# State space branch with features on partitions and its norm applied later; first weights in contiguous blocks; key rotation issued between the halves of the query latent

## The chip, the cores and the metric

The kernel runs on one core of a Trainium2 chip. A core has five engines that work side by side and meet through semaphores: TensorE (PE, matrix products; its weight loads are shown apart as PEld), VectorE (DVE), ScalarE (ACT), GpSimd (POOL) and SyncE (SP, which here only issues DMAs). Data lies in SBUF, a memory of 128 partitions; products land in PSUM, in banks of 128 partitions by 512 floats. Each engine works through its own list of instructions in order.

The metric is the device time of one execution, in microseconds (us). Times are medians of several runs; a profile is one further execution.

## The reference: what is computed

Two layers of a decoder trunk on 512 tokens of width 1024, in float32. In each layer a normed input goes through one wide projection, whose columns feed three branches: a state space scan (Mamba-2 SSD), latent attention (MLA) and a gated delta rule (GDN). Each branch is projected to the model's width and weighted by a sigmoid gate; their sum goes through an output projection and a feed-forward part. The branch that the change is about, cut to what matters:

```python
def ssd_mixer(z, xbc, dt_raw, conv_w, conv_b, dt_bias, a_log, d_skip, norm_g):
    xbc = silu(causal_dwconv(xbc, conv_w) + conv_b)
    xs, bm, cm = split(xbc)                       # 16 heads of 64; 2 groups of 8 heads; state 128
    dt = softplus(dt_raw + dt_bias)
    a = -exp(a_log)
    y = ssd_chunked(xs * dt[..., None], dt * a, bm, cm)
    y = y + d_skip[:, :, None] * xs
    y = y * silu(z)
    return rmsnorm(y, norm_g)                     # over the 512 features of each group

def ssd_chunked(X, dA, Bm, Cm):                   # chunks of 128 tokens
    A_cum = cumsum(dA)
    L = exp(where(tril, A_cum[l] - A_cum[s], -inf))
    CB = einsum('ln,sn->ls', Cc, Bc)
    y_diag = einsum('ls,ls,sp->lp', CB, L, X)
    states = einsum('ln,l,lp->pn', Bc, exp(A_cum[-1] - A_cum), X)
    # scan over the chunks: h = h * exp(A_cum[-1]) + states
    y_off = einsum('ln,pn,l->lp', Cc, h_prev, exp(A_cum))
    return y_diag + y_off
```

## The kernel before

**Number formats.** The large (dense) products are three products each (`mm3`, L182 to L184) of operands split in a high and a low part of type fp32r. A weight tile comes from DRAM by a DMA on SP's queue (`weights_raw`, L161, two buffers `wraw`), ACT casts the high part (`split_half`, L154), DVE subtracts it for the low part (L155). The small products of the scans are plain fp32. `dense_F` makes a product with features on the output's partitions (weights held in the array, 512 tokens streaming), `silu_T`'s product has tokens on the partitions (token blocks held, 512 weight columns streaming).

**Buffers.** PSUM has four banks `acc` for dense products, three banks `sm` for small ones and one, `yt`. SBUF tiles come from pools with a fixed number of buffers by name: `tok` (four of 128x2048), `eE` (four), `wk0` to `wk3` (one each), `ft4` (two), `st` (two). A tile that takes a buffer over waits until its last reader is done.

**Order.** The program is written stage by stage, and a scheduler reorders each engine's list by priority and by readiness; weights' casts are marked as high priority. So the list of PE holds dense products of the next stage between the small products of a scan. Around the SSD branch the program has, in each layer: `ssd_group(0)`, the decays of the delta rule (`gdn_decays`, which uses `seg_exp` and the `eE` buffers too, and writes `d_e`), half of the attention's output projection, `ssd_group(1)`, the other half, `gdn_matrix` for two halves of the heads, `gdn_blocks` (inverses of 32x32 blocks on DVE, by way of DRAM: `d_n`, then `d_x`, which PE waits for at L891), the SSD branch's output projection with steps of the inverse (L891 to L929) between its rows, then the rest of the delta rule.

**The SSD branch.** `step_sizes` makes the cumulative sums `cum`, stores them as rows in DRAM (`d_c`), and exponentials of them (`dec`), the step `dtq` and the skip factor `dsk`. One call of `ssd_group(g)` does 8 heads:

- Projections of B, C (features on partitions), and of x in two 256-wide pieces (features on partitions), convolved (`conv`), then transposed by PE (L720) and copied by ACT (L721) so that `xs` has tokens on partitions; z by `silu_T` with tokens on partitions.
- For each of the four chunks t: `seg_exp` loads the chunk's cumulative sums of four heads into an `eE` buffer, broadcast to all partitions (L448, 256 KB), and ACT takes the exponentials (L450, L451); twice for 8 heads. PE makes C·B (L733), DVE masks it (L735) and multiplies it into both `eE` (L737). `xd` is x times the step (L739). Eight products `py` (L742) hold a head's 128x128 decay matrix in the array and stream its 64 columns of `xd`. `y` is the skip term (L744) plus `py` (L745). For t > 0 the state's share `po` (L748, the C block held, the state's 512 columns streaming) is scaled by `dec` (L750) and added (L751). For t < 3 the state is brought forward (L754, L756, L759 to L762). y is multiplied into `z` (L764), and ACT squares it and sums along the row (L766).
- At the end POOL takes the root (`rsq`, L258 and L259), DVE scales the four rows of z (L770), PE transposes all of it (L775) and `split_gain` (ACT L254, DVE L255) applies the gain and makes the high and low parts `yh`, `yl` for the output projection.

**The attention's start.** `query_latent(0)` and `(1)` project the query's latent in two halves, and sums of its squares come from PE (L513). `rope` rotates the key: four DMAs on ACT's queue copy it with halves swapped (L519 to L521), DVE multiplies by cosine and sine. The queries' own rotations come later and end in `qps` (L591), which the scores (L625) read.

**Loads at the start of a layer.** `front_raw` (L306 to L310) loads the weights of the first small projections, four pieces of 128 x 704, each row a piece of a longer row in DRAM.

Of the kernel before, what the change touches and what calls it, by code (L numbers as in the profile page):

```python
# [10 lines left out]
F32 = mybir.dt.float32  # L11
# [9 lines left out]
P = 128  # L21
# [13 lines left out]
ROWS = ('ssd_dt_bias', 'gdn_dt_bias', 'ssd_a_log', 'gdn_a_log', 'ssd_d')  # L35
# [20 lines left out]
def hybrid_kernel(ctx, tc, a, out, depth=2, taps=None):  # L56
# [4 lines left out]
    def mk(pl, shape, dt, tag, bufs=None):  # L61
        return pl.tile(shape, dt, tag=tag, name=f"{tag}_{next(uid)}", bufs=bufs)
# [30 lines left out]
    def sm_bank():  # L93
        return mk(ps_sm, [P, 512], F32, "sm")
# [4 lines left out]
    ct = mk(cst, [P, NBLK * P + 104], F32, "ct")  # L99
# [195 lines left out]
    def load_params(ly, rows=True):  # L295
        pc = mk(sp, [P, 155], F32, "pc", 2)
        sync.dma_start(pc, a["pcols"][ly])
        prow = mk(sp, [P, 64], F32, "prow", 2)
        if rows:
            load_rows(prow, ly)  # L300
        return pc, prow
# [49 lines left out]
    for ly in range(depth):  # L351
# [5 lines left out]
        sconv_b, g_n1, g_ssd, g_q, g_kv, g_gdn, g_n2 = 0, 12, 20, 28, 32, 34, 35  # L357
# [32 lines left out]
        d_c = mk(dr, [T, 24 * P], F32, "d_c", 2)  # L390

        def step_sizes():
# [35 lines left out]
            sync.dma_start(d_c.rearrange("t (n l) -> (t n) l", l=P), rows)  # L428
            dec = mk(sp, [P, 3, T, 24], F32, "dec")
# [8 lines left out]
            dsk = mk(sp, [P, 16], F32, "dsk")  # L438
            dve.tensor_scalar(dsk, prow[:, 48:64], 0.25, None, ALU.mult)
# [63 lines left out]
        query_latent(0)  # L503
        ckh, ckl = latent(lp, ck_tok, 256, g_kv, "ck")
        ps = sm_bank()
        for t in range(T):
            pe.transpose(ps[:, t * P : (t + 1) * P], kr_tok[:, t], ident)
        kd = mk(lp, [P, S], F32, "mix", 8)
        act.copy(kd, ps)
        query_latent(1)  # L510
        ps = sm_bank()
        for t in range(T):
            pe.matmul(ps[:, t : t + 1], cq_sq[0][:, t * P : (t + 1) * P], ones[:, 0:1], start=True, stop=True)  # L513
        q_rs = mk(sp, [P, T], F32, "qrs")
        rsq(q_rs, ps[:, :T], 1.0 / 512, EPS)

# [10 lines left out]

        kpe = rope(kd)
# [4 lines left out]
        dve.tensor_tensor(kps[64:], kpe[64:], f32(kph[64:]), ALU.subtract)  # L533

# [162 lines left out]
        def ssd_group(g, yh, yl):  # L697
            h0 = 8 * g
            xs = mk(br, [P, T, 512], F32, "tok", 4)
            z = mk(br, [P, T, 512], F32, "tok", 4)  # L700
# [13 lines left out]
            for cp in range(2):  # L714
                for j, pj in enumerate(dense_F(weights(w_in, O_XBC + 512 * g + 256 * cp, 256, D), tiles(256), D, xh, xl)):
                    xf = mk(br, [P, S], F32, "ft4", 2)
                    conv(pj, 4 * g + 2 * cp + j, xf)
                    ps = sm_bank()
                    for t in range(T):
                        pe.transpose(ps[:, t * P : (t + 1) * P], xf[:, t * P : (t + 1) * P], ident)  # L720
# [4 lines left out]
            ss = mk(sp, [P, T], F32, "sss")  # L725
            st = None
            for t in range(T):
# [10 lines left out]
                xd = mk(br, [P, 512], F32, "wk0")  # L738
                dve.tensor_tensor(hv8(xd), hv8(xs[:, t, :]), bc_last(dtq[:, t, h0 : h0 + 8], 64), ALU.mult)  # L739
                py = sm_bank()  # L740
                for h in range(8):
                    pe.matmul(py[:, h * 64 : (h + 1) * 64], e2[h // 4][:, h % 4, :], xd[:, h * 64 : (h + 1) * 64], start=True, stop=True)  # L742
                y = mk(br, [P, 512], F32, "wk1")
                dve.tensor_tensor(hv8(y), hv8(xs[:, t, :]), bc_last(dsk[:, h0 : h0 + 8], 64), ALU.mult)  # L744
                dve.tensor_tensor(y, y, py, ALU.add)  # L745
                if t > 0:
                    po = sm_bank()
                    pe.matmul(po, ctl[:, tok], st, start=True, stop=True)  # L748
                    y2 = mk(br, [P, 512], F32, "wk2")
                    dve.tensor_tensor(hv8(y2), hv8(po), bc_last(dec[:, 0, t, h0 : h0 + 8], 64), ALU.mult)  # L750
                    dve.tensor_tensor(y, y, y2, ALU.add)  # L751
                if t < T - 1:
                    xe = mk(br, [P, 512], F32, "wk3")
                    dve.tensor_tensor(hv8(xe), hv8(xd), bc_last(dec[:, 1, t, h0 : h0 + 8], 64), ALU.mult)  # L754
                    pst = sm_bank()
                    pe.matmul(pst, btok[:, t, :], xe, start=True, stop=True)  # L756
# [7 lines left out]
                dve.tensor_tensor(z[:, t, :], z[:, t, :], y, ALU.mult)  # L764
                jk = mk(br, [P, 512], F32, "wk2")
                act.activation(jk, z[:, t, :], AF.Square, accum_out=ss[:, t : t + 1])  # L766
            rs = mk(sp, [P, T], F32, "srs")
            rsq(rs, ss, 1.0 / 512, EPS)
            for t in range(T):
                dve.tensor_scalar(z[:, t, :], z[:, t, :], rs[:, t : t + 1], None, ALU.mult)  # L770
            for c in range(4):
                k = 4 * g + c
                ps = y_bank()
                for t in range(T):
                    pe.transpose(ps[:, t * P : (t + 1) * P], z[:, t, c * P : (c + 1) * P], ident)  # L775
                split_gain(yh[k], yl[k], ps, col(g_ssd + k))
                tap(f"yssd{k}", f32(yh[k]))
# [24 lines left out]
        def gdn_matrix(u):  # L802
# [26 lines left out]
            nt = mk(br, [P, T, 4, P], F32, "tok", 4)  # L829
# [14 lines left out]
        def gdn_blocks():  # L844
# [4 lines left out]
            wk = mk(br, [P, 2, 32, 32], F32, "tok", 4)  # L849
# [20 lines left out]
        def gdn_inverse(ms, blocks):  # L870
# [4 lines left out]
            X = mk(br, [P, 2, 4 * T, 64], F32, "tok", 4)  # L875
# [63 lines left out]
        def gdn_unit(u, kT, ork, cc, cd, Yt, yh, yl):  # L939
# [18 lines left out]
            v = mk(br, [P, T, 512], F32, "tok", 4)  # L958
            gz = mk(br, [P, T, 512], F32, "tok", 4)
# [314 lines left out]
def lay_out(inputs):  # L1274
# [4 lines left out]
    cols = np.concatenate([v[n].reshape(depth, -1, P) for n in PARAMS], axis=1)  # L1279
# [4 lines left out]
    res["w_front"] = np.ascontiguousarray(w.reshape(depth, KD, P, NF).transpose(0, 2, 1, 3)).reshape(depth, P, KD * NF)  # L1284
# [18 lines left out]
```

## Time and profile before

| | |
|---|---|
| median of 3 runs | 2335.56 us (2330.37 to 2335.94) |
| the profiled execution | 2337.45 us |
| its span, first to last instruction | 2335.7 us |
| mean granted TensorE clock | 0.994 of full speed |
| mean share of the DMA engines' time on q1 (the loads) | 33.0% |

The page divides the span in 40 slices. Each digit below is the busy share of one slice in tenths.

```profile
PE   8999999999999999999999999999999999999998
DVE  7776657765675458767767765667756645677668
ACT  5666744333443345545656667443334434545545
PEclk9999999989999999999999999999999999999999
DMA  4223533442322443233132235334423224333231
```

A busy PE is not PE at its peak: matmuls overlap and their ends are modelled, so the durations in the groups add up to more than the time they take. Where a time per matmul is needed, the distance from one start to the next is the better number. The page counts an fp32 product as two records.

### The profile page before, as it was taken

How to read it: one execution, taken by the hardware profiler on the slowest of the kernel's cores; microseconds unless marked ns; L12 is line 12 of the kernel's file. 1: busy time of each engine (PE TensorE's matmuls, PEld its weight loads, DVE VectorE, ACT ScalarE, POOL GpSimd, SP SyncE). 2: the span in 40 equal slices, each digit the busy share in tenths (PEclk: the TensorE clock that was granted, in tenths of full speed). 3: DMA queues.
4: the chain of work that ended last, by engine and by line, in shares of the span. 5: the costliest groups of instructions: out<-in, count | busy, mean ns of one | idle time of the engine just before them, and what ended most of it. 6: DMA issues, size and time to landing. Idle time of an engine off the chain costs nothing.

```text
span 2335.7 us, 32023 instructions
## 1 busy us (share of the span) xinstructions
PE 2294.3 (98%) x11814; PEld 1889.9 (81%) x11814; DVE 1586.4 (68%) x3116; ACT 1177.1 (50%) x2455; POOL 59.5 (3%) x74
## 2 busy tenths in 40 slices
PE   8999999999999999999999999999999999999998
PEld 7878788878887888888888787888788878888886
DVE  7776657765675458767767765667756645677668
ACT  5666744333443345545656667443334434545545
POOL 0000000000000000000010000000000000000000
PEclk9999999989999999999999999999999999999999
DMA  4223533442322443233132235334423224333231
GB/s 136 83 69 91 171 100 111 117 136 73 86 75 66 146 152 101 72 126 115 41 106 68 82 92 170 100 106 138 118 82 86 68 78 157 127 117 100 90 109 46
DMA packets 208703, 239.85 MB, mean 103 GB/s; under 512 B 33889, under 2 KB 157473, under 8 KB 208545
## 3 DMA queue, kind: packets, MB, share of 16 engines
q1 hardware_dynamic: 205344, 233.07, 33.0%
q10 hardware_dynamic: 3200, 4.72, 0.8%
q8 instruction: 93, 1.52, 0.3%
q14 instruction: 66, 0.53, 0.1%
HBM read 221.41 MB, written 11.63 MB: 100 GB/s over the span
## 4 chain that ended last, share of the span: by engine, by line
PE 88%; DVE 6%; DMA 2%; ACT 2%; POOL 1%; issue 1%; ACTq 0%; SPq 0%; DVEq 0%; POOLq 0%
PE acc L182 23%; PE acc L184 22%; PE acc L183 22%; PE sm L184 2%; PE sm L182 2%; PE sm L183 2%; DVE wlo L155 1%; PE sm L742 1%; DMA eE<-d_c 1%; PE sm L645 1%; DVE tok L858 1%; DVE gQ L857 1%; PE sm L1015 1%; POOL gms L259 1%; PE yt L661 1%
## 5 line engine op out<-in xcount | busy, mean ns | idle before, releaser
L155 DVE TENSOR_TENSOR wlo<-wraw,whi 128x512 fp32r<-128x512 f32 (+1 forms) x552 | 376.6, 686 | 420.8 <-ACT whi L154 401.5
L154 ACT CAST whi<-wraw 128x512 fp32r<-128x512 f32 (+1 forms) x552 | 339.9, 618 | 593.1 <-PE acc L183 383.6
L184 PE MATMUL acc<-xh,wlo 128*128 128x512 f32 (+1 forms) x1248 | 486.8, 390 | 0.0
L182 PE MATMUL acc<-xh,whi 128*128 128x512 f32 (+1 forms) x1248 | 486.1, 390 | 0.0
L183 PE MATMUL acc<-xl,whi 128*128 128x512 f32 (+1 forms) x1248 | 485.1, 389 | 0.0
L184 PEld LDWEIGHTS acc<-xh,wlo 128*128 128x128 f32 x1248 | 235.8, 189 | 44.9 <-issue 0.3
L183 PEld LDWEIGHTS acc<-xl,whi 128*128 128x128 f32 x1248 | 235.8, 189 | 44.4 <-DVE xl L255 0.4
L182 PEld LDWEIGHTS acc<-xh,whi 128*128 128x128 f32 x1248 | 235.3, 189 | 43.7 <-ACT xh L254 0.4
L182 PE MATMUL acc<-yh,whi 128*128 128x512 f32 x384 | 151.9, 399 | 0.0
L183 PE MATMUL acc<-yl,whi 128*128 128x512 f32 x384 | 151.4, 394 | 0.0
L184 PE MATMUL acc<-yh,wlo 128*128 128x512 f32 x384 | 151.2, 394 | 0.0
L686 DVE SCALAR_TENSOR_TENSOR ckl<-acc,pc,ckl 128x511 f32<-128x511 f32 (+2 forms) x168 | 120.2, 743 | 15.5 <-ACT ckl L682 8.2
L154 ACT CAST whi<-wr 128x512 fp32r<-128x512 f32 x128 | 79.5, 621 | 66.7 <-PE acc L184 31.1
L184 PE MATMUL acc<-whi,xl 128*128 128x512 f32 (+1 forms) x288 | 111.2, 386 | 0.0
L183 PE MATMUL acc<-wlo,xh 128*128 128x512 f32 (+1 forms) x288 | 111.1, 386 | 0.0
L182 PE MATMUL acc<-whi,xh 128*128 128x512 f32 (+1 forms) x288 | 110.3, 385 | 0.0
L182 PE MATMUL acc<-whi,yh 128*128 128x512 f32 x256 | 99.7, 389 | 0.0
L184 PE MATMUL acc<-whi,yl 128*128 128x512 f32 x256 | 99.7, 389 | 0.0
L183 PE MATMUL acc<-wlo,yh 128*128 128x512 f32 x256 | 99.6, 389 | 0.0
L155 DVE TENSOR_TENSOR wlo<-wr,whi 128x512 fp32r<-128x512 f32 x128 | 86.0, 686 | 12.2 <-ACT whi L154 11.4
L182 PEld LDWEIGHTS acc<-yh,whi 128*128 128x128 f32 x384 | 71.7, 188 | 16.7 <-ACT yh L254 1.7
L183 PEld LDWEIGHTS acc<-yl,whi 128*128 128x128 f32 x384 | 72.2, 188 | 15.2 <-issue 1.0
(418 smaller groups left out, 4531.0 us busy)
## 6 DMA issues: line engine op xcount, KB each, us to landing
wraw<-in_w_in_dram SPq DMA_DIRECT2D x144, 512.0 KB, 3.6
wraw<-in_w_up_dram SPq DMA_DIRECT2D x64, 512.0 KB, 3.6
wr<-in_w_down_dram SPq DMA_DIRECT2D x32, 1024.0 KB, 5.0
eE<-d_c SPq DMA_DIRECT2D x48, 256.0 KB, 3.9
wraw<-in_w_mla_out_dram SPq DMA_DIRECT2D x16, 512.0 KB, 3.4
eE<-d_e SPq DMA_DIRECT2D x32, 256.0 KB, 3.2
wraw<-in_w_ssd_out_dram SPq DMA_DIRECT2D x16, 512.0 KB, 3.4
wraw<-in_w_gdn_out_dram SPq DMA_DIRECT2D x16, 512.0 KB, 3.3
```

Of the source, the lines that this page charges most:

```text
L154: act.copy(hi, raw)
L155: dve.tensor_tensor(lo, raw, f32(hi), ALU.subtract)
L182: pe.matmul(o, ah, bh, start=start, stop=False, skip_group_check=more)
L183: pe.matmul(o, ah, bl, start=False, stop=False, skip_group_check=more)
L184: pe.matmul(o, al, bh, start=False, stop=stop, skip_group_check=more)
L259: pool.tensor_tensor(o, o, (exp if exp is not None else nhalf)[:, : o.shape[1]], ALU.pow)
L645: pe.transpose(ps[:, n : n + P], pn[t][:, kb * P : (kb + 1) * P], ident)
L661: pe.matmul(o, v_h, th[:, c : c + w], start=kb == 0, stop=False)
L686: dve.scalar_tensor_tensor(acc[:, d:], ps[:, : S - d], taps_[3 - d], acc[:, d:], ALU.mult, ALU.add)
L742: pe.matmul(py[:, h * 64 : (h + 1) * 64], e2[h // 4][:, h % 4, :], xd[:, h * 64 : (h + 1) * 64], start=True, stop=True)
L857: dve.tensor_tensor(pd, bc_last(nb[:, m, m + 1 :], m + 1), bc_mid(xb[:, m, : m + 1], 31 - m), ALU.mult)
L858: dve.tensor_tensor(xb[:, m + 1 :, : m + 1], xb[:, m + 1 :, : m + 1], pd, ALU.add)
```

## The change

Three things change. The sums and products that make up the output stay the same, in another layout.

1. *The SSD branch keeps features on partitions.* The convolved x stays as it is (`xf`), is scaled by the skip factor in place (a column per feature now, read from the parameters), and its transpose goes from PSUM straight into `xd`, multiplied by the step. z is projected by `dense_F`. The products `py` hold a head's 128x64 piece of `xd` and stream the decay matrix; odd heads write PSUM partitions 64 to 127. `po` is four products. The factor exp(cum), which was a scalar per partition, now varies along the row, and is loaded from a new DRAM tile `d_p` into the buffers `wk0` and `wk1`. The sum of squares over features is now a sum over partitions, made by two adds on DVE and a product with ones into the bank `yt`. The root goes to DRAM (`d_r`) and comes back broadcast in the function `normed`, which multiplies z by gain and root and splits it. `normed` is called after the attention's output projection for the first group, and between the two calls of `gdn_matrix` for the second. `tok` gets a fifth buffer.
2. *The first weights* lie in DRAM as four contiguous blocks per layer.
3. *The key's rotation* is issued before `query_latent(1)`, not after it.

```diff
-        sync.dma_start(raw, a["w_front"][ly][:, 2 * q * NF : 2 * (q + 1) * NF])
+        sync.dma_start(raw, a["w_front"][ly, q])
...
+            prows = mk(ml, [96, P], F32, "crowe")
+            act.activation(prows, pc_[:96, :P], AF.Exp)
+            sync.dma_start(d_p.rearrange("t (n l) -> (t n) l", l=P), prows)
...
-            dsk = mk(sp, [P, 16], F32, "dsk")
-            dve.tensor_scalar(dsk, prow[:, 48:64], 0.25, None, ALU.mult)
+            dsk = mk(sp, [P, 8], F32, "dsk")
+            dve.tensor_scalar(dsk, pc[:, 112 + c_d : 120 + c_d], 0.25, None, ALU.mult)
...
+        kd = mk(lp, [P, S], F32, "mix", 8)
+        act.copy(kd, ps)
         kpe = rope(kd)
...
+        query_latent(1)
...
-            xs = mk(br, [P, T, 512], F32, "tok", 4)
-            z = mk(br, [P, T, 512], F32, "tok", 4)
+            xf, xd, z = (mk(br, [P, T, 512], F32, "tok", 5) for _ in range(3))
...
-                    act.copy(xs[:, :, (2 * cp + j) * P : (2 * cp + j + 1) * P], ps.rearrange("p (t n) -> p t n", t=T))
-            silu_T(br, O_SZ + 512 * g, z)
+                    dve.tensor_tensor(th(xd[:, :, c * P : (c + 1) * P]), th(ps.rearrange("p (t n) -> p t n", t=T)),
+                                      bc_last(dtq[:, :, h0 + 2 * c : h0 + 2 * c + 2], 64), ALU.mult)
+                    act.activation(xf[:, c, :], xf[:, c, :], AF.Copy, scale=dsk[:, 4 * g + c : 4 * g + c + 1])
+            for cp in range(2):
+                for j, pj in enumerate(dense_F(weights(w_in, O_SZ + 512 * g + 256 * cp, 256, D), tiles(256), D, xh, xl)):
+                    silu2(z[:, 2 * cp + j, :], pj)
...
+            pss = y_bank()
...
-                for h in range(8):
-                    pe.matmul(py[:, h * 64 : (h + 1) * 64], e2[h // 4][:, h % 4, :], xd[:, h * 64 : (h + 1) * 64], start=True, stop=True)
-                y = mk(br, [P, 512], F32, "wk1")
-                dve.tensor_tensor(hv8(y), hv8(xs[:, t, :]), bc_last(dsk[:, h0 : h0 + 8], 64), ALU.mult)
-                dve.tensor_tensor(y, y, py, ALU.add)
+                for c in range(4):
+                    for i in range(2):
+                        h = 2 * c + i
+                        pe.matmul(py[64 * i : 64 * i + 64, c * P : (c + 1) * P], xd[:, t, h * 64 : (h + 1) * 64], e2[h // 4][:, h % 4, :], start=True, stop=True)
+                y = xf[:, :, tok]
+                dve.tensor_tensor(y, y, c4(py), ALU.add)
                 if t > 0:
+                    eb = mk(br, [P, 4, P], F32, f"wk{t % 2}")
+                    for i in range(2):
+                        sync.dma_start(eb[64 * i : 64 * i + 64], d_p.rearrange("t (n l) -> t n l", l=P)[t, h0 + i : h0 + 8 : 2].partition_broadcast(64))
                     po = sm_bank()
-                    pe.matmul(po, ctl[:, tok], st, start=True, stop=True)
...
+                    for c in range(4):
+                        pe.matmul(po[:, c * P : (c + 1) * P], st[:, c * P : (c + 1) * P], ctl[:, tok], start=True, stop=True)
+                    dve.tensor_tensor(eb, c4(po), eb, ALU.mult)
+                    dve.tensor_tensor(y, y, eb, ALU.add)
...
-                jk = mk(br, [P, 512], F32, "wk2")
-                act.activation(jk, z[:, t, :], AF.Square, accum_out=ss[:, t : t + 1])
+                zt = z[:, :, tok]
+                dve.tensor_tensor(zt, zt, y, ALU.mult)
+                sq = mk(br, [P, 4, P], F32, "wk2")
+                act.activation(sq, zt, AF.Square)
+                dve.tensor_tensor(sq[:, 0:2], sq[:, 0:2], sq[:, 2:4], ALU.add)
+                dve.tensor_tensor(sq[:, 0], sq[:, 0], sq[:, 1], ALU.add)
+                pe.matmul(pss[:, t : t + 1], sq[:, 0], ones[:, 0:1], start=True, stop=True)
...
-            for t in range(T):
-                dve.tensor_scalar(z[:, t, :], z[:, t, :], rs[:, t : t + 1], None, ALU.mult)
-            for c in range(4):
-                k = 4 * g + c
-                ps = y_bank()
-                for t in range(T):
-                    pe.transpose(ps[:, t * P : (t + 1) * P], z[:, t, c * P : (c + 1) * P], ident)
-                split_gain(yh[k], yl[k], ps, col(g_ssd + k))
+            sync.dma_start(d_r[g].rearrange("(t p) -> p t", p=P), rs)
+
+            def normed():
+                rb = mk(br, [P, S], F32, "ft4", 2)
+                sync.dma_start(rb, d_r[g].partition_broadcast(P))
+                for c in range(4):
+                    k = 4 * g + c
+                    dve.scalar_tensor_tensor(z[:, c, :], z[:, c, :], col(g_ssd + k), rb, ALU.mult, ALU.mult)
+                    split_act(yh[k], yl[k], z[:, c, :])
...
-        ssd_group(0, *ys)
+        normed = [ssd_group(0, *ys)]
         gdn_decays()
         out_proj(a["w_mla_out"][ly], 1, *y_mla, br, (0, 1))
-        ssd_group(1, *ys)
+        normed.append(ssd_group(1, *ys))
         out_proj(a["w_mla_out"][ly], 1, *y_mla, br, (2, 3))
+        normed[0]()
...
-        mats = [gdn_matrix(u) for u in range(2)]
+        mats = [gdn_matrix(0)]
+        normed[1]()
+        mats.append(gdn_matrix(1))
```

`split_act` (L248 to L251, there already) copies the high part on ACT and subtracts it on DVE.

More of the change, by code (lines that the diff above doesn't have):

```diff
@@ L295, in load_params @@
     def load_params(ly, rows=True):
[L296 removed]
+        pc = mk(sp, [P, 163], F32, "pc", 2)
         sync.dma_start(pc, a["pcols"][ly])
[L298 removed]
+        prow = mk(sp, [P, 48], F32, "prow", 2)
         if rows:
@@ L389, in hybrid_kernel @@
         cum = mk(sp, [P, T, 24], F32, "cum")
-        d_c = mk(dr, [T, 24 * P], F32, "d_c", 2)
+        d_c, d_p = (mk(dr, [T, 24 * P], F32, n, 2) for n in ("d_c", "d_p"))
+        d_r = mk(dr, [2, S], F32, "d_r", 2)
         def step_sizes():
@@ L526, in rope @@
             return ta
+        query_latent(0)
+        ckh, ckl = latent(lp, ck_tok, 256, g_kv, "ck")
+        ps = sm_bank()
+        for t in range(T):
+            pe.transpose(ps[:, t * P : (t + 1) * P], kr_tok[:, t], ident)
+        kd = mk(lp, [P, S], F32, "mix", 8)
+        act.copy(kd, ps)
         kpe = rope(kd)
@@ L533, in hybrid_kernel @@
         dve.tensor_tensor(kps[64:], kpe[64:], f32(kph[64:]), ALU.subtract)
+        query_latent(1)
+        ps = sm_bank()
+        for t in range(T):
+            pe.matmul(ps[:, t : t + 1], cq_sq[0][:, t * P : (t + 1) * P], ones[:, 0:1], start=True, stop=True)
+        q_rs = mk(sp, [P, T], F32, "qrs")
+        rsq(q_rs, ps[:, :T], 1.0 / 512, EPS)
         pts = [mk(ml, [P, S], F32R, f"pt{i}") for i in range(2)]
@@ L828, in gdn_matrix @@
                                   bc_last(rk2[:, i, :], 2), ALU.mult)
-            nt = mk(br, [P, T, 4, P], F32, "tok", 4)
+            nt = mk(br, [P, T, 4, P], F32, "tok", 5)
             for t in range(T):
@@ L844, in gdn_blocks @@
         def gdn_blocks():
-            wk = mk(br, [P, 2, 32, 32], F32, "tok", 4)
+            wk = mk(br, [P, 2, 32, 32], F32, "tok", 5)
             nb, xb = wk[:, 0], wk[:, 1]
@@ L870, in gdn_inverse @@
         def gdn_inverse(ms, blocks):
-            X = mk(br, [P, 2, 4 * T, 64], F32, "tok", 4)
+            X = mk(br, [P, 2, 4 * T, 64], F32, "tok", 5)
             th = range(4 * T)
@@ L957, in gdn_unit @@
                 act.copy(ktok[i].rearrange("p t n -> p (t n)"), ps)
-            v = mk(br, [P, T, 512], F32, "tok", 4)
-            gz = mk(br, [P, T, 512], F32, "tok", 4)
+            v = mk(br, [P, T, 512], F32, "tok", 5)
+            gz = mk(br, [P, T, 512], F32, "tok", 5)
             for i in range(2):
```

47 lines of the change are left out of this document (16 added, 31 removed).

## The prediction

> **What bounds the kernel now.** I read the page first: busy time, then the chain that ended last, then the waits of PE.
>
> ```profile
> PE 2294.3 (98%) x11814; PEld 1889.9 (81%) x11814; DVE 1586.4 (68%) x3116; ACT 1177.1 (50%) x2455; POOL 59.5 (3%) x74
> PE 88%; DVE 6%; DMA 2%; ACT 2%; POOL 1%; issue 1%; ACTq 0%; SPq 0%; DVEq 0%; POOLq 0%
> PE sm L625 <- ACT qps L591: 4.4, 3, 1.9
> PE sm L891 <- DMA wk<-d_x: 3.2, 2, 2.2
> PE yt L1046 <- DVE tok L1041: 2.9, 4, 0.9
> PE yt L775 <- DVE tok L770: 1.3, 2, 0.7
> ```
>
> TensorE is busy for 98% of the span, and the chain is 88% PE. The waits (total us, times, longest) are small: the scheduler puts dense products of the next stage between the steps of the scan. So nearly every edit is worth what it takes from or gives to PE's stream, unless it makes PE wait. The scan (SSD) stage is not quite so simple, as the chain in order of time (start, us) shows for the first group of layer 0:
>
> ```profile
> 253.17 1.98 PE sm L742 x16
> 255.21 3.84 DMA eE<-d_c
> ...
> 262.97 1.09 PE sm L742 x8
> 264.07 4.07 DMA eE<-d_c
> ```
>
> Here a loop shares the path: the y products (L742) release the decay buffers, which are loaded again (eE<-d_c), go through the exponents on ACT and the multiply on DVE, and feed the y products two chunks on. A faster PE does not shorten that loop.
>
> **The change, PE part by part.** Durations come from one execution of 2337.45 us (span 2335.7, so 1.75 around it), 1.9 above the runs' median of 2335.56. A gain is worked out against the former and carried to the median as it is. Matmul durations overlap, so I price by start-to-start steps, from the timeline (start, duration):
>
> ```profile
> 237.81 0.39 PE L184 MATMUL acc<-xh,wlo 128*128 128x512 f32 x1
> 238.04 1.06 PE L742 MATMUL sm<-wk,eE 128*128 128x64 f32 x8
> ...
> 240.89 0.48 PE L182 MATMUL acc<-xh,whi 128*128 128x512 f32 x1
> 241.21 0.39 PE L183 MATMUL acc<-xl,whi 128*128 128x512 f32 x1
> ...
> 244.41 1.90 PE L742 MATMUL sm<-wk,eE 128*128 128x64 f32 x16
> 246.14 1.08 PE L748 MATMUL sm<-st,ckh 128*128 128x512 f32 x2
> 247.06 1.02 PE L756 MATMUL sm<-wk,kt 128*128 128x512 f32 x2
> ```
>
> A run of 16 L742 records takes 246.14 − 244.41 = 1.73, 0.11 each; a pair of L748 takes 0.92, 0.46 each. An fp32 matmul leaves two records, two passes, as the groups' counts show (8 y products in each of 16 chunks are 128 instructions, 256 records):
>
> ```profile
> L742 PE MATMUL sm<-wk,eE 128*128 128x64 f32 x256 | 31.9, 273 | 2.0 <-DVE eE L737 1.9
> L775 PE MATMUL yt<-ct,tok 128*128 128x128 f32 x64 | 10.9, 277 | 1.3 <-DVE tok L770 1.3
> L947 PE MATMUL sm<-ct,ft 128*128 128x1 f32 x64 | 7.5, 242 | 0.0
> 655.44 1.68 PE sm L947 x16
> 401.95 0.60 PE L775 MATMUL yt<-ct,tok 128*128 128x128 f32 x4
> ```
>
> 1. Transposes of the gated y (L775) go: 64 records. Four take 0.60, of which 0.27 is the last one's own length, so the step is (0.60 − 0.27)/3 = 0.11: −7.0. Their wait for the scaled rows goes too: −1.3.
> 2. New sums of squares through ones: 16 instructions, 32 passes. L947 has the same shape (128x1): 1.68/16 = 0.105, so +3.4.
> 3. The state's share of y (L748; three chunks of each of four groups, 24 passes) becomes four 128-wide products for one 512-wide: 24 × 0.46 = 11.0 becomes 96 × 0.11 = 10.6, −0.4.
> 4. The 256 passes of y now hold a 128x64 piece of x still and stream the 128 columns of the decay matrix, odd heads going to the lower half of PSUM. As one stream they cost 256 × 0.11 = 28.2, as before. Odd and even heads sit on different column halves of the array and may run together. No row of before shows two tiles that differ by columns alone; the nearest are the 64x64 products that differ by rows and columns:
>
> ```profile
> 540.80 0.22 PE L927 MATMUL sm<-tok,tok 64*64 64x64 f32 x1
> 540.81 0.22 PE L929 MATMUL sm<-tok,kt 64*64 64x64 f32 x1
> 540.86 0.22 PE L927 MATMUL sm<-tok,tok 64*64 64x64 f32 x1
> ...
> 541.57 0.22 PE L929 MATMUL sm<-tok,kt 64*64 64x64 f32 x1
> 541.72 0.50 PE L182 MATMUL acc<-yh,whi 128*128 128x512 f32 x1
> 542.05 0.39 PE L183 MATMUL acc<-yl,whi 128*128 128x512 f32 x1
> 528.25 0.39 PE L184 MATMUL acc<-xh,wlo 128*128 128x512 f32 x1
> 528.57 1.14 PE L927 MATMUL sm<-tok,tok 64*64 64x64 f32 x16
> ```
>
> Two passes start 0.01 apart and the pair repeats after 0.06: full overlap. So the bounds for y are 28.2 (none) and 14.1 (full); I take full, plus 1.7 for passes without a partner (in the compiled order four of nine runs of each group hold an odd number of y products: 4 runs × 4 groups × 2 passes × 0.055).
>
> Those runs are 36 visits to the halved array, and a visit is not free. Into L927 the step from L184 is 528.57 − 528.25 = 0.32, while L184 to L742 above took 0.23: 0.09. Out of it, L929 to L182 takes 0.15 where a pair needs 0.06: 0.09. The first dense step after is 0.33, but 0.32 after plain fp32 too (240.89 to 241.21): 0.01. So 0.19 each, 36 × 0.19 = 6.8; the bounds are 0 and 0.34, as if the whole of the three delays were new (12.2 in all). y together: 14.1 + 1.7 + 6.8 − 28.2 = −5.6.
>
> The Trainium skill, "TensorEngine Tiling (Array Packing)", section Performance Considerations, advises this very swap where the streamed side is 64 wide and promises up to two times; section Key Properties says that a change of mode drains the engine. By the first alone y would be −14.1; the exit and entry rows above are the drain of the second.
>
> 5. z is projected with weights held still in two 256-wide pieces instead of four token blocks: 96 dense products per group either way, 0.23 each, no change; the smaller rows (1 KB for 2 KB) load weights that are not waited for, as the casts show, whose idle time ends with PE giving a buffer back:
>
> ```profile
> L154 ACT CAST whi<-wraw 128x512 fp32r<-128x512 f32 x544 | 336.4, 620 | 592.2 <-PE acc L183 383.6 <-PE acc L184 110.7 <-PE yt L183 25.1
> L154 ACT CAST mix<-wraw 128x352 fp32r<-128x352 f32 x8 | 3.8, 484 | 1.7 <-PE acc L183 1.5 <-DMA wraw<-in_w_front_dram 0.2
> L154 ACT CAST whi<-wraw 128x352 fp32r<-128x352 f32 x8 | 3.5, 482 | 0.9 <-DMA wraw<-in_w_front_dram 0.8
> ```
>
> **Beside PE.** The contiguous first weights can save at most the 0.2 + 0.8 of these casts, and lose nothing that is waited for: 0. On DVE the x·dt multiply moves to the projections, the skip product goes to ACT as a scaling of the convolved columns; two narrow adds per chunk come in, the four scalings L770 of a group become multiplies by the broadcast norm, and the four scaled subtracts behind the transposes (L255) become plain ones:
>
> ```profile
> L744 DVE TENSOR_TENSOR wk<-tok,dsk 128x512 f32<-128x512 f32 x16 | 11.0, 684 | 0.0
> L766 ACT ACTIVATE wk<-tok 128x512 f32<-128x512 f32 x16 | 10.0, 624 | 8.0 <-DVE tok L764 8.0
> L770 DVE TENSOR_SCALAR tok<-tok,srs 128x512 f32<-128x512 f32 x16 | 6.7, 482 | 3.4 <-POOL srs L259 3.4
> 267.15 0.38 SPq L161 DMA_DIRECT2D wraw<-in_w_mla_out_dram  x1
> ```
>
> Per group −4 × 0.68 (skip), +4 × 2 × 0.68 at most (the adds are a half and a quarter as wide as L744), +4 × (0.68 − 0.48), the subtracts alike: at most +3.5 us, on an engine busy for 68% of the span: 0. The per-chunk factors and the norm arrive by DMA, 24 + 4 loads and 6 small stores on SP's queue, 0.38 of issue each (the wraw row), 13 us in all on a queue with room. Where one waits for its buffer or for POOL's root, the weight loads queued behind it start 3 to 5 us later, and PE is not served late while the casts wait for PE (the row above). Without that cover it would be those 3 to 5 us in each of four groups.
>
> The key's rotation is issued earlier; the wait at L625 is for qps, the query's copy, so it stays: 0, bounds −1 and +2 for the reshuffled order there.
>
> **Waits that come in.** Sums of squares stand inside PE's in-order stream, behind the y add, gate multiply, Square and the two adds: four DVE steps of at most 0.68 and 0.62 on ACT, at most 3.3 us, and 4.7 with the state's share. The order gives about ten to twenty dense products (2.3 to 4.6 us) before each, so it is near balance; all later matmuls queue behind a late one. Also the loop of the exponents keeps its length while PE gets shorter: on the chain it holds about half of the chunks. I take half of y's 5.6 for both, +3 rounded; bounds 0 and 16 × 1.5 (L625's mean wait, 4.4/3), 24.
>
> Sum: −7.0 − 1.3 + 3.4 − 0.4 − 5.6 + 3 = −7.9. From the profiled 2337.45 that is 2329.6, from the median 2327.7: **2328 us**.
>
> **Rivals.**
> - *All of it pays* (0.15): overlap full, switches free, nothing late: −7.0 − 1.3 + 3.4 − 0.4 − 12.4 = −17.7, 2318. For: the 0.06 pair. Against: the 0.15 exit.
> - *The loop of loads and exponents takes over* (0.17): y's gain all turns into PE waiting for eE: −5.3, 2330. For: two eE loads on the chain above. Against: other groups' chain is mostly PE.
> - *The columns don't overlap* (0.17): both halves share the rows that feed them. Then +6.8 to +12.2 for y: −5.3 + 6.8 = +1.5, or +6.9: 2337 to 2342. For: no column-only pair in the trace. The change then does not do what it says for PE.
> - *The sums of squares stall PE* (0.17, the slower side): at the 16 places PE waits 1.5 us each: −10.9 + 24 = +13, 2349. It decides from 18/16 = 1.1 us per place. For: L1046 waits 0.7 (2.9/4) behind a DVE chain. Against: the dense products ahead.
> - Clock, within each of these. In layer 0 the wait of 2.2 at L891 is followed by half clock:
>
> ```profile
> 480.00:520.00 40.00, 37.84 (x344) 30.78 (x345) 29.12 (x66) 14.30 (x24) 0.00 (x0) 0.88 0.52 135
> 520.00:560.00 40.00, 40.00 (x386) 32.00 (x378) 17.19 (x27) 13.76 (x24) 0.00 (x0) 0.95 0.23 66
> ```
>
> 40 × 0.12 + 40 × 0.05 = 6.8 us lost. A new wait of that size costs as much, a shorter one at L891 gives it back. The Trainium skill, "TensorE: Matmul & The Clock Gate", section Why this matters for your kernels, puts the limit at about 3 us of idle; here 2.2 sufficed, so the trace decides.
>
> **How the numbers follow.** The forecast has 0.34. Faster or slower means by over 0.3% (7 us, about what a measurement of this kernel can tell from no change): below 2328.5 or above 2342.6. Faster: 0.15 of the first, 0.20 of the forecast, 0.09 of the loop (where the clock drop goes): 0.44. Slower: the stalls 0.17, the dear end of no overlap 0.05: 0.22. Same: 0.34. The range runs from 2316 to 2345, which leaves out most of the stall case and the first's lower tail; the forecast's own is 2324 to 2333.
>
> **What would show it.** L775 gone; y records starting in pairs, 256 in about 16 us, or 0.11 apart if they don't overlap; 36 gaps of 0.2 around them; waits of PE at the sums of squares under 0.3 each; the eE loads still on the chain; L625 and L891 waiting as before. Wrong it is if PE's waits in the scan stage grow beyond 10 us, if y keeps 0.11 a pass, or if the half-clock stretches change in number.

## The result and the profile after

| | us |
|---|---|
| before, median of 4 runs beside the changed kernel | 2335.75 (2330.37 to 2342.27) |
| changed kernel, median of 4 | 2352.82 (2349.73 to 2354.41) |
| ratio, 95% interval | 1.0077 (1.0062 to 1.0092) |
| forecast | 2328, range 2316 to 2345 |

The changed kernel is 17 us slower where 8 us of gain were forecast. First its page: the busy times and the chain that ended last.

```profile
PE 2292.5 (97%) x11854; PEld 1880.1 (80%) x11854; DVE 1586.5 (67%) x3132; ACT 1172.8 (50%) x2441; POOL 58.9 (3%) x74
PE 83%; DVE 6%; DMA 5%; ACT 3%; issue 1%; POOL 1%; ACTq 0%; SPq 0%; DVEq 0%; POOLq 0%
PE acc L182 21%; PE acc L183 21%; PE acc L184 21%; PE sm L182 2%; PE sm L184 2%; PE sm L183 2%; DVE wlo L155 1%; DMA d_e<-eE 1%; DMA eE<-d_c 1%; PE sm L751 1%; DMA d_r<-srs 1%; ACT whi L154 1%; DVE tok L876 1%; PE sm L649 1%; ACT eE L454 1%
```

TensorE's busy time hardly moved (2294.3 before). Its share of the chain fell from 88% to 83%, and what came in is DMA, 2% to 5%, with two stores by name: `d_e<-eE` and `d_r<-srs`. The waits of PE (total us, times, longest) say the same from the other side:

```profile
PE acc L184 <- DVE wlo L155: 7.5, 4, 1.9
PE sm L629 <- ACT qps L595: 5.6, 3, 2.1
PE acc L182 <- ACT whi L154: 5.5, 5, 1.6
PE sm L715 <- DVE ft L263: 5.0, 2, 2.8
```

Three of these rows have no counterpart in the waits of before: dense products waiting for their weights' low and high parts (13.0 us), and the transposes of B waiting for a convolution that such products feed (5.0).

Where the time is lost can be read off the chain in order of time (start, us, what), by the start of the same products in both kernels. Before; L742 x8 are the first y products of a group, L812 x12 open the delta rule:

```profile
238.20 0.90 PE sm L742 x8
...
354.94 0.90 PE sm L742 x8
...
429.26 1.34 PE sm L812 x12
...
1398.95 0.90 PE sm L742 x8
...
1516.14 0.91 PE sm L742 x8
...
1590.85 1.34 PE sm L812 x12
```

After, with the same products at L751 and L830, and the DMAs on the chain between them:

```profile
238.91 1.02 PE sm L751 x16
...
270.54 14.32 DMA d_e<-eE
...
366.57 1.02 PE sm L751 x16
...
397.00 10.33 DMA d_r<-srs
...
440.53 1.34 PE sm L830 x12
...
1403.96 1.02 PE sm L751 x16
...
1436.07 14.10 DMA d_e<-eE
...
1531.61 1.02 PE sm L751 x16
...
1562.31 8.67 DMA d_r<-srs
...
1607.47 1.34 PE sm L830 x12
```

The lag is 0.7 at the first group and 11.6 at the second; 5.0 and 15.5 in layer 1. So each layer loses 10 to 11 us between its two groups, around the end of the first one. From the second group to the delta rule the lag stays (11.6 to 11.3, 15.5 to 16.6), though the second group's 16 transposes have gone there. Between 440 and 1404 some 6 us come back, and that goes with the clock: before, the stretch from 500 to 560 us had a mean clock of 0.89, after 1.00 (60 x 0.11 = 6.6). No run shows that the change brought this about.

What happens at the end of the first group is seen in the windows around it (stretch, its length, then busy us and instructions of PE, PEld, DVE, ACT and POOL; clock, DMA share, GB/s). After:

```profile
262.00:270.00 8.00, 8.00 (x42) 6.39 (x43) 4.74 (x9) 4.26 (x10) 1.01 (x1) 1.00 0.79 247
270.00:280.00 10.00, 10.00 (x46) 8.29 (x45) 2.67 (x4) 5.03 (x15) 0.00 (x0) 1.00 0.23 24
280.00:290.00 10.00, 6.49 (x23) 4.68 (x22) 3.34 (x5) 1.95 (x5) 0.00 (x0) 0.81 0.68 197
```

The DMA engines move 247 GB/s until 270 and 24 GB/s in the ten us after. Before, the same ten us had 228 GB/s:

```profile
270.00:280.00 10.00, 9.32 (x43) 7.22 (x42) 4.72 (x10) 7.39 (x21) 1.01 (x1) 1.00 0.79 228
```

TensorE goes on for those ten us with weights that are already there and then runs dry: 6.49 us busy of the next ten, and a mean clock of 0.81 on top. What was issued at 270 is in SyncE's queue:

```profile
269.52 0.38 SPq L784 DMA_DIRECT2D d_r<-srs  x1
269.95 0.50 SPq L161 DMA_DIRECT2D wraw<-in_w_mla_out_dram  x1
270.54 1.64 SPq L818 DMA_DIRECT2D d_e<-eE  x2
280.18 0.32 SPq L788 DMA_DIRECT2D ft<-d_r  x1
284.92 0.32 SPq L452 DMA_DIRECT2D eE<-d_c  x1
```

The first is the store of the root: 512 values, each alone in its place because token t·128 + p lies on partition p. The list of issues (KB each, us to landing) gives its landing:

```profile
d_r<-srs SPq DMA_DIRECT2D x4, 2.0 KB, 10.2
```

2 KB take 10 us, where the loads of weights (512 KB) and of `eE` (256 KB) take 3 to 4 in the same list. The weight load issued right after it, at 269.95, is told by the view of that line alone:

```profile
L161 SPq DMA_DIRECT2D wraw<-in_w_mla_out_dram x1: 499/499/499, 269.9 to 269.9; - x1
  ACT whi L154: 9.1, 1
DMA to landing us min/median/max: 14.2/14.2/14.2
```

It lands after 14.2 us, and the cast waits 9.1 for it. The two `d_e` stores behind it are the 14.32 of the chain, and the next loads into `eE` wait for those. SyncE meanwhile stands, first at the load of the root, then at the load into `eE`, so that the next weight load is issued only at 286.24. So weights come late in two ways here: one lands late, the next ones are issued late.

### The profile page after: what moved, and what is told of

Its sections match the earlier page's. It is cut to its first block, busy times and chain, and to the rows that moved or that the text cites. A ratio compares the mean times of both kernels' runs of the same rounds, so it can differ in the third digit from the quotient of the medians.

```text
span 2352.6 us, 32151 instructions
## 1 busy us (share of the span) xinstructions
PE 2292.5 (97%) x11854; PEld 1880.1 (80%) x11854; DVE 1586.5 (67%) x3132; ACT 1172.8 (50%) x2441; POOL 58.9 (3%) x74
## 4 chain that ended last, share of the span: by engine, by line
PE 83%; DVE 6%; DMA 5%; ACT 3%; issue 1%; POOL 1%; ACTq 0%; SPq 0%; DVEq 0%; POOLq 0%
PE acc L182 21%; PE acc L183 21%; PE acc L184 21%; PE sm L182 2%; PE sm L184 2%; PE sm L183 2%; DVE wlo L155 1%; DMA d_e<-eE 1%; DMA eE<-d_c 1%; PE sm L751 1%; DMA d_r<-srs 1%; ACT whi L154 1%; DVE tok L876 1%; PE sm L649 1%; ACT eE L454 1%
## 5 line engine op out<-in xcount | busy, mean ns | idle before, releaser
L184 PE MATMUL acc<-xh,wlo 128*128 128x512 f32 (+1 forms) x1376 | 536.5, 390 | 0.0
L182 PE MATMUL acc<-xh,whi 128*128 128x512 f32 (+1 forms) x1376 | 535.6, 390 | 0.3 <-ACT whi L154 0.3
L183 PE MATMUL acc<-xl,whi 128*128 128x512 f32 (+1 forms) x1376 | 534.5, 389 | 0.0
L184 PEld LDWEIGHTS acc<-xh,wlo 128*128 128x128 f32 x1376 | 259.5, 189 | 50.2 <-DVE wlo L155 0.7
L182 PEld LDWEIGHTS acc<-xh,whi 128*128 128x128 f32 x1376 | 259.3, 189 | 49.7 <-ACT whi L154 0.7
L183 PEld LDWEIGHTS acc<-xl,whi 128*128 128x128 f32 x1376 | 259.6, 189 | 49.1 <-DVE xl L255 0.4
L184 PEld LDWEIGHTS acc<-yh,wlo 128*128 128x128 f32 x384 | 73.4, 191 | 25.0 <-DVE wlo L155 10.2
L454 ACT ACTIVATE eE<-eE,cum 128x128 f32<-128x128 f32 x192 | 63.1, 390 | 29.4 <-DMA eE<-d_c 23.3
L1236 DVE TENSOR_TENSOR h<-h,acc 128x512 f32<-128x512 f32 x96 | 61.5, 679 | 0.0
```

The lines of the kernel that those rows point to most:

```text
L182: pe.matmul(o, ah, bh, start=start, stop=False, skip_group_check=more)
L183: pe.matmul(o, ah, bl, start=False, stop=False, skip_group_check=more)
L184: pe.matmul(o, al, bh, start=False, stop=stop, skip_group_check=more)
L454: act.activation(o[:, i], o[:, i], AF.Relu, scale=-1.0, bias=cum[:, t, h0 + i : h0 + i + 1])
L1236: dve.tensor_tensor(hs_, hs_, ps[t], op)
```

## The experiments

Theory A: the scattered store holds up all DMA for some 10 us, four times, and the late weights are the loss. Theory B: the store's shape is harmless; SyncE standing at the load of the broadcast root, or the other new loads, make the weights late. The key's rotation was a third suspect, and the parts of the forecast's sum that lie on PE were to be measured by themselves. Ratios are against before on the same chip, with 95% intervals.

### The root stored by rows

```diff
-            sync.dma_start(d_r[g].rearrange("(t p) -> p t", p=P), rs)
+            pr = sm_bank()
+            pe.transpose(pr[:T, :P], rs, ident)
+            rrow = mk(sp, [T, P], F32, "rrow")
+            act.copy(rrow, pr[:T, :P])
+            sync.dma_start(d_r[g].rearrange("(t p) -> t p", p=P), rrow)
```

> The changed kernel, but the root is transposed by TensorE first and leaves as four rows of 512 bytes, not as 512 pieces of 4 bytes. Theory A (the scattered store holds up all DMA queues for some 10 us, four times): the weight loads behind it land in 4 to 5 us again, TensorE's waits for weight casts after each group go, and the time falls by 20 to 28 us from 2352.8, to 2325 to 2333 us. Theory B (SyncE's queue standing at the load of the root's broadcast, or the other new loads, delays the weights, whatever the store's shape): 2348 us or more, and the waits for casts stay.

Measured: 2327.24 us, 0.9968 (0.9956 to 0.9979). That is 26 us under the changed kernel and faster than before. Of PE's waits, the first row and that of the new transpose:

```profile
PE sm L629 <- ACT qps L595: 5.6, 3, 2.1
...
PE sm L785 <- POOL srs L259: 2.3, 4, 0.6
```

The rows for casts are gone from the list; the one wait of the new transpose for POOL's root costs 0.6 a time. A holds, and B as it was put falls: SyncE's queue still has the load of the root, and it delays nothing that PE waits for. But the shape also changes how long SyncE stands at that load: from 270.5 to 271.9 in the first group here, from 272.2 to 280.2 in the changed kernel. So this run shows that the scattered store is the cause, and not how much of the loss goes by SyncE's standing.

### The store alone, on the kernel before

```diff
             rsq(rs, ss, 1.0 / 512, EPS)
+            sync.dma_start(d_r[g].rearrange("(t p) -> p t", p=P), rs)
```

> The kernel before with nothing of the change but the scattered store of the root (its result is read by nobody). Theory A: the store takes about 10 us to land, the weight load next to it lands 10 us late, and the time rises by 8 to 25 us over 2335.7. Theory B: within 3 us of before, since nothing waits for the store.

Measured: 2353.42 us, 1.0079 (1.0058 to 1.0100), 18 us more for four stores of 2 KB that nobody reads. They land after 9.8 to 10.6 us, and two new waits head PE's list, one for a cast, one of the transposes of the gated y for DVE:

```profile
PE acc L182 <- ACT whi L154: 5.6, 3, 2.9
PE yt L777 <- DVE yl L255: 5.2, 2, 2.6
```

The expectation had the weight load next to the store land late. In the second group it does: issued at 396.51, 3 us behind the store, it lands after 11.1 us. In the first group no weight load is near the store, and SyncE's queue shows another way:

```profile
271.31 0.37 SPq L770 DMA_DIRECT2D d_r<-srs  x1
271.77 0.46 SPq L802 DMA_DIRECT2D d_e<-eE  x1
281.72 0.32 SPq L449 DMA_DIRECT2D eE<-d_c  x1
282.14 0.39 SPq L161 DMA_DIRECT2D wraw<-in_w_mla_out_dram  x1
```

The `d_e` store behind the scattered one lands after 12.1 us, SyncE waits 9.5 us for it at the load that takes over its buffer, and the weight load behind that is issued at 282.14 (before: 273.99). So SyncE stands here too, though the queue has no load of the root.

### Fewer and larger pieces

`rearrange("(p t) -> p t", t=T)` in place of `"(t p) -> p t"` in that store, so that a partition's four values make one piece of 16 bytes.

> e2_store_alone with the root laid out in DRAM so that each partition's four values are one piece: 128 pieces of 16 bytes, not 512 of 4 bytes. If each small piece costs alike: landing in 3 to 4 us against 10, and 2336 to 2340 us. If it is a fixed cost of storing from 128 partitions: 10 us again, and 2348 to 2355.

Measured: 2331.47 us, 0.9991 (0.9978 to 1.0005), where before took 2331.92 on that chip: free. The landing:

```profile
DMA to landing us min/median/max: 1.4/1.6/4.2
```

By the medians a quarter of the pieces takes less than a sixth of the time (1.6 against 10.0), so it is not a fixed cost of storing from 128 partitions, nor one price for each piece whatever its size. Whether it is the size of 4 bytes or the number 512 was not separated.

### The store on another queue

`act.dma_start` for `sync.dma_start` in the store alone.

> e2_store_alone with the scattered store issued from ScalarE's queue. If the pieces hold up the DMA engines themselves: weight loads of SyncE's queue beside it land 8 to 10 us late as before, 2346 to 2356 us. If they hold up only the queue that they were issued on: the weight loads land in 4 to 5 us, 2335 to 2340 us.

Measured: 2342.00 us, 1.0038 (1.0023 to 1.0053). The store, on ScalarE's queue, takes nearly as long, and a weight load issued on SyncE's queue 3 us after the second store waits as well. Its view, after the store's:

```profile
L770 ACTq DMA_DIRECT2D d_r<-srs x4: 366/368/394, 269.7 to 1550.8; - x4
DMA to landing us min/median/max: 8.3/9.0/9.2
```

```profile
L161 SPq DMA_DIRECT2D wraw<-in_w_mla_out_dram x1: 383/383/383, 392.9 to 392.9; - x1
...
DMA to landing us min/median/max: 9.9/9.9/9.9
```

So the hold-up crosses queues: it is in something that they share. From 389 to 399 us the core's DMA engines moved 11 GB/s at a busy share of 0.11 (before: 107 and 0.36). By the profile the engines are not busy then, so whether the pieces wait in the engines or at the memory behind them is not shown. The time lies between the two expectations, and why it costs half as much in the end (9 against 18 us) is not settled.

### Store and load, on the kernel before

The store alone, and behind it the load of its broadcast into an `ft4` buffer.

> e2_store_alone with the load of the root's broadcast behind the store, on SyncE's queue as in the changed kernel; its result is read by nobody. e2_store_alone stands at 1.0079 of before. If SyncE standing at a load that waits for the slow store delays what is queued behind it further: 1.010 to 1.013, which with the gain of the rest (e1_row_store, 0.9968) gives the changed kernel's 1.0077. If the engines held up are all there is to it: 1.007 to 1.009.

Measured: 2359.06 us, 1.0097 (1.0070 to 1.0124). The middle lies between the two expectations and the interval reaches into both. Its four runs spread over 12 us and were granted clocks of 0.990 to 0.996, before beside them 0.994 to 0.999, so a part of the difference may be the clock. Not decided.

### Rows and store together

The kernel that stores by rows, with the scattered store added into a tile `d_q` that nobody reads.

> e1_row_store, which stores the root by rows, with the scattered store added, written to a place that nobody reads. The changed kernel stands at 1.0077 of before, e1_row_store at 0.9968. If the store alone makes the whole difference: 1.0065 to 1.009. If a part of it comes from SyncE standing at the load that waits for the store: 1.003 to 1.006, as e2_store_alone's 0.8% on top of e1_row_store would give.

Measured: 2339.15 us, 1.0029 (1.0015 to 1.0043). The store costs 14 us more here as well (1.0029 − 0.9968 = 0.0061), just under the second expectation, and does not reach the changed kernel's 1.0077. The rest is 0.5%. SyncE's standing from 272.2 to 280.2 at the load that needs the store (the queue shown above) looks like the suspect, but this run did not take such standing out: in the first group SyncE stands from 273.4 to 280.8 at a load into `eE`, in the second from 392.1 to 399.9 at the load of the root, since the store by rows behind the scattered one is held up with it. This kernel's queue also has a weight load placed otherwise. That split stays open; both parts go with the scattered store.

### The key's rotation

Alone on the kernel before, and taken out of the changed kernel; then taken out of the kernel that stores by rows.

```diff
         act.copy(kd, ps)
-        kpe = rope(kd)
...
         query_latent(1)
...
         rsq(q_rs, ps[:, :T], 1.0 / 512, EPS)
+        kpe = rope(kd)
```

> The kernel before with the key's rotation moved and nothing else. If the move costs: 2338 to 2340 us, with the new wait of 1.4 us for the query's low part in layer 0. If it does not: 2335 to 2336, within the spread of before.

> The changed kernel with the key's rotation back behind the second half of the query latent. In the changed kernel TensorE is 3 us later at the end of layer 0's attention than at its start, against before, with a new wait of 1.4 us and a half-clock stretch of 3.4 us there. If the moved rotation causes that: 2349 to 2351 us, and both are gone. If it is only the other order of the program: 2352 to 2355.

> The row-wise store of e1_row_store and the key's rotation behind the second half of the query latent, as before. e3_key_back was 5.6 us faster than the changed kernel, e4_key_alone changed nothing on the kernel before. If the rotation's place costs by itself in the changed program: 2321 to 2324 us, below e1_row_store's 2327.2. If those 5.6 us hung on the attention's waits falling the other way by a hair (a half-clock stretch more or less): within 2 us of 2327.

Measured: alone 2334.60, 1.0001 (0.9989 to 1.0014). Taken out of the changed kernel 2347.22, 1.0057 (1.0036 to 1.0077), faster than either expectation, with an interval that overlaps the changed kernel's. Taken out of the row-wise kernel 0.9970 (0.9957 to 0.9983), against 0.9968 with it. The move costs nothing that can be measured; the one run in which it seemed to is not borne out by the other two.

### The first weights alone

```diff
-        sync.dma_start(raw, a["w_front"][ly][:, 2 * q * NF : 2 * (q + 1) * NF])
+        sync.dma_start(raw, a["w_front"][ly, q])
```

> The kernel before with the first weights in contiguous blocks and nothing else. All theories: within 1 us of before, since the casts of these weights wait 1.0 us for them in all; a loss of 3 us or more would make it a part of the result.

Measured: 2333.20, 1.0001 (0.9989 to 1.0013). Nothing, as expected.

### No pairs on the column halves

```diff
-                for c in range(4):
-                    for i in range(2):
+                for i in range(2):
+                    for c in range(4):
                         h = 2 * c + i
```

> e1_row_store with the eight y products of a chunk in the order of the even heads, then the odd ones, so that only one neighbouring pair of a chunk lies on different column halves. If the halves run together (a chunk's 8 products take 4 steps of two passes at 0.11 when paired, and 7 when not): 16 chunks x 3 steps x 2 passes x 0.11 = 10.6 us more, 2336 to 2339 us. If pairs don't overlap, or TensorE is not what bounds there: 2327 to 2329.

Measured: 1.0003 (0.9993 to 1.0013), that is 0.35% or 8 us above the row-wise kernel. Both timelines show it in the first chunk. With pairs, in the row-wise kernel:

```profile
236.24 1.09 PE L751 MATMUL sm<-eE,tok 128*64 128x128 f32 x16
237.27 1.12 PE L767 MATMUL sm<-wk,kt 128*128 128x512 f32 x2
```

Without:

```profile
237.12 1.58 PE L751 MATMUL sm<-eE,tok 128*64 128x128 f32 x16
238.63 1.12 PE L767 MATMUL sm<-wk,kt 128*128 128x512 f32 x2
```

16 passes take 1.03 with pairs, where 16 of before took 1.73, and 1.51 without. Sixteen chunks at 0.48 each are 7.7 us, near the 8 that were measured. (The 10.6 expected took 0.66 per chunk.) So products on halves of the array that differ by columns alone ran together here.

### The sums last

The four products for the sums of squares moved behind the group's last chunk (a tile `s1` keeps the added squares), which leaves 28 runs of y products for 36.

> e1_row_store with the four products for the sums of squares after the group's last chunk, from a tile that keeps the added squares. The runs of y products are 28 in place of 36. If a change of array halves costs 0.19 us: 1.5 us less, 0.996 of before, which the interval can hardly tell from e1_row_store's 0.9968; if the products stood in TensorE's way more than that: 0.995 or less.

Measured: 2325.68, 0.9967 (0.9955 to 0.9979), no difference in the total from the row-wise kernel. But the total hides one. The table takes from each profiled execution two stretches, one per layer, from the start of the first y product to that of the delta rule's first product (L812 of before); nearly all that the change moves on TensorE lies in them. The view of windows with these ends gives length, TensorE's idle time (length less busy time) and mean clock, in us:

| kernel | layer 0 | layer 1 | sum | idle | clock |
|---|---|---|---|---|---|
| before | 191.06 | 191.90 | 382.96 | 3.3 | 1.00, 1.00 |
| changed | 201.53 | 203.42 | 404.95 | 19.1 | 0.97, 0.97 |
| root stored by rows | 189.00 | 188.80 | 377.80 | 3.5 | 1.00, 1.00 |
| by rows, no pairs | 192.13 | 192.00 | 384.13 | 3.5 | 1.00, 1.00 |
| by rows, sums last | 186.02 | 186.62 | 372.64 | 2.4 | 1.00, 1.00 |
| by rows and scattered store | 193.71 | 195.28 | 388.99 | 8.5 | 0.99, 0.98 |

The three kernels that add only the key's move, the first weights or the 16-byte store to before take 382.5 to 383.7 in the same stretches, so some 1 us is noise. At full clock in both, the kernel with the sums last is 5.2 us shorter than the row-wise one. In its profiled execution the clock took that back elsewhere: 0.66 over the 15 us behind the wait for `d_x` in either layer, where the row-wise kernel had 1.00. Its ten runs were granted 0.994 to 0.999, those of the row-wise kernel 0.997 or 0.998. So the products between the chunks did stand in TensorE's way. Little of that is waiting (1.1 us of idle time). One place shows the loss: in the row-wise kernel two passes of a run of eight start at 240.91, the sum's two at 241.25, the other six at 241.56 and the next product at 242.14. That is 1.23 us, where an unbroken run of eight takes 0.59 (249.57 to 250.16). How much of the 5.2 is such breaks and how much the new order of TensorE's list was not separated.

The fastest here are the row-wise kernels with paired heads, all at 0.997 of before, whichever place the key or the sums have.

## Why the prediction was wrong

The step that failed is in the part beside PE: "24 + 4 loads and 6 small stores on SP's queue, 0.38 of issue each", where the stores have no price but issue, and "the weight loads queued behind it start 3 to 5 us later", which was the whole bound on lateness. The four stores of the root cost no issue to speak of and 10 us of landing each, and what was issued behind them came late with them. The load behind one started on time, at 269.95, and landed 14.2 us later; the one after it was issued at 286.24, where before had issued it at 273.99, some 12 us later and not 3 to 5. The cover that I named (casts that wait for PE to give a buffer back) lasted for the ten us in which PE still ran. The prediction had a price without that cover, 3 to 5 us in each of four groups, but gave that case no chance and no place among the rivals. I counted the store by its issue; its row of 512 single values was in the diff, and the trace of before has no store of that kind to price it by. A bound for its landing was due there, and I set none. The sign that I had set for being wrong, waits of PE in the scan stage grown beyond 10 us, came: its idle time in the two stretches of the table grew from 3.3 to 19.1 us.

The other steps, by the row-wise kernel, which has the change without that store:

- *The sum*, −7.9, met 7.5 us of 2335 (0.9968; 5 to 10 by the interval), with one more small transpose per group. That agreement is in part luck. In the two stretches of the table the row-wise kernel gains 5.2 us. The rest goes with the clock: its eight runs were granted 0.997 to 0.998, and the two runs of before beside them that were granted 0.998 took 2331.1 and 2331.8, some 4 us above its 2327.24. That the change brought the better clock is not shown.
- *Overlap of column halves*: right. The changed kernel's y passes come at 1.02 us for 16, and the pairs are worth 8 us by the runs, 6.3 in the stretches.
- *A visit to the halved array* at 0.19: not confirmed; with eight visits fewer the stretches took 5.2 us less, where 1.5 was expected.
- *The sums of squares stall PE*, the rival on the slower side: wrong as it was put. In the changed kernel's groups of PE the last column is the idle time before them, and the sums (L781) have 0.1 in all, the y products 1.0:

```profile
L781 PE MATMUL yt<-ct,wk 128*128 128x1 f32 x32 | 5.6, 244 | 0.1
L751 PE MATMUL sm<-eE,tok 128*64 128x128 f32 x256 | 23.5, 284 | 1.0 <-ACT whi L154 0.4 <-DVE eE L746 0.4
```

What the sums cost is TensorE's own time: where they stand between the y products, their term of +3.4 was too small, by up to 5.2.
- *Waits that come in*, +3: mis-sized. The row-wise kernel has 2.3 at its added transpose, and the y products wait 0.4 where they waited 1.9 before, about +0.8. With it the sum would be −7.9 − 2.2 = −10.1. The kernel with the sums last has −10.3 in the two stretches, the row-wise one −5.2: what is missing there goes with the place of the sums of squares.
- *The loop of loads and exponents takes over*: the eE loads are still on the changed kernel's chain, at 1% as before; no run tried the loop by itself.
- *Key rotation and first weights* at 0: right.
- *The clock*: the prediction let the size of the wait at L891 decide, and these traces don't bear that out. With only the key's rotation moved, a wait of 2.09 there left the clock at 1.00 over the 15 us behind it; with the sums last, one of 1.12 was followed by 0.66. Runs of before on one chip were granted 0.994 to 0.999 and took from 2340.75 down to 2327.90 us, so some us of any difference here can be the clock. In the changed kernel its new half-speed stretches follow dry spells such as the one at 285 us; the row-wise kernel, without the scattered store, has 1.00 there. They are worth about 12 us (405 × 0.03) in the two stretches.

So the slower side came true by a mechanism that was not among the rivals.

## What to carry to other kernels

Price a store by the pieces that it falls into, not by its bytes: a vector whose neighbours lie on different partitions and that must leave in token order is better transposed on TensorE first (here a product of 0.27 us, a wait of up to 0.6 and a small copy) than scattered. A small DMA that is slow to land can cost far more than its own reader's wait; look at what is issued in the ten us behind it, and at what the issuing engine stands at. Where a new transfer has no row in the trace before, set a bound for its landing, and ask what starves if it takes that long. When a difference is a few us in 2335, compare the stretch in which the change lies, at the same granted clock, before the totals.

## What was not expected of the hardware

A store of 512 single 4-byte values from 128 partitions took 7.8 to 11.6 us to land in these traces, from SyncE's or ScalarE's queue, and other transfers slowed meanwhile: in ten us with the store the core's DMA engines moved 24 GB/s where before moved 228 (store on SyncE's queue), or 11 where before moved 107 (on ScalarE's). The same 2 KB as 128 pieces of 16 bytes landed in 1.4 to 4.2, with a median of 1.6.

A product with one streamed column, put between two parts of a run of 128x64 products, cost about 0.64 us (1.23 against 0.59), where its two passes were priced at 0.21 and the further visit to the halved array at 0.19.
